# Two of the three modulation parts computed by VectorE from transposed weights, x^T loaded last, experts' biases split on 128 partitions

## The chip, the core and the metric

One core of a Trainium2 chip runs the whole kernel in one launch. The metric is the device time of a launch in microseconds (us). The kernel before takes 1138.96 us (median of 3 runs, 1138.25 to 1139.63).

## The reference

One decoder layer on 256 tokens of width 1024, all in float32. Six vectors of width 1024 (a shift, a scale and a gate for each half of the layer) come from a condition vector `c`; they modulate the inputs of a token mixer and of a mixture of 32 experts, of which each token takes 4.

```
mod = silu(c) @ w_ada + b_ada                    # 1024 -> 6 * 1024
sh_a, sc_a, g_a, sh_f, sc_f, g_f = split(mod, 6)
h   = x * (1 + sc_a) + sh_a
mix = hybrid_mixer(h, w_in, ...)                 # sparse attention and retention, then w_out
x   = layer_norm(ALPHA * x + (1 + g_a) * mix)
h   = x * (1 + sc_f) + sh_f
ff  = moe(h, w_router, w_gate_up, b_gate_up, w_down, b_down)   # top 4 of 32 experts
out = layer_norm(ALPHA * x + (1 + g_f) * ff)
```

## The kernel before

The kernel has a head (modulation, mixer, router) and a body (the 32 experts, whose 12 MB of weights each are streamed from HBM). All large loads are issued by SyncE (SP) in program order as tiles of 128 x 2048 floats, 1 MB each. In the head they go through a ring of 6 buffers (`rtile`, name `w`): a load is issued only when the tile that had the buffer before has been read. In the body 17 buffers (the ring and 11 others, most of which are scratch space of the head) take the experts' tiles in turn. TensorE (PE), VectorE (DVE), ScalarE (ACT) and GpSimd (POOL) each work through a queue of their own in a fixed order, which a scheduler sets at build time from the program order and estimated times; only the end of the kernel and TensorE's part of the router are written out by hand.

**Modulation.** `w_ada` (1024 x 6144) is cut into three parts of 2048 columns and each part into 8 row blocks of 128 (`mod_step(part, k)`). A step loads a 1 MB tile and multiplies it on TensorE with the condition: 4 matmuls of 512 columns into four row groups of one PSUM bank (`pm`). `mod_row` adds the bias, and `mod_cols` transposes the row on TensorE (`pmt`), since the shift and the scale are wanted as one number for each channel, with channels on partitions. Part 0 (shift and scale of the mixer) is needed before anything else: its 8 tiles are loaded first, with x^T behind the sixth. Parts 1 and 2 are spread through the head by `mod_next`, two steps (MODS) ahead of a tile of `w_in`.

**Projections.** x^T (`xT`) is modulated to `h` and split into a rounded part `hh` and a rest `hl` (fp32r). Each tile of `w_in` is split too (`split`): ScalarE makes the rounded part `whi`, VectorE the rest `wlo` (GpSimd for tiles 2, 6 and 10). A projection is three groups of matmuls, `whi` with `hh`, `whi` with `hl`, `wlo` with `hh`, so that its last third waits for `wlo`. There is a small first tile (`w_idx`, 544 columns) and 12 tiles of `w_in`: tile 0 for the index queries, 1 and 2 for the attention queries (`pq`), 3 for keys and values (`pk`), 4 to 7 for the retention queries and keys (`pr`, `rotary`), 8 to 11 for its values and gate (`pv`). Beside them VectorE does the scores (L350), the choice of 64 keys of 256 by eight rounds of MAX and MATCH_REPLACE for each token block (L356, L357), the rotary products (L398 to L401), and the softmax. Then come the output projection (`pz`, 4 tiles of `w_out`), the layer norm and the router (`pg` gathers the tokens for the first experts).

**Biases of the experts.** `bias_rows` loads the biases three times over on 96 partitions and splits them into three bfloat16 parts with one conversion by ScalarE and four instructions by VectorE for each of the two tensors.

Of the kernel before, what the change touches and what calls it, by code (L numbers as in the profile page):

```python
# [23 lines left out]
MODS = 2  # L24
# [4 lines left out]
def layouts(inputs):  # L29
# [20 lines left out]
    head = np.concatenate([ident, cols(g["c"]), cols(g["b_ada"][:2048])], 1)  # L50
# [24 lines left out]
    for c in (2116, 2628):  # L75
# [18 lines left out]
def layer(ctx, tc, t, out):  # L94
# [41 lines left out]
    small(out=dec, in_=t["row"])  # L136
# [5 lines left out]
    ones = sb("ones", 128, 128, pool=keep)  # L142
    G.memset(ones, 1.0)
# [3 lines left out]
    G.memset(epsc, EPS)  # L147

# [6 lines left out]
    b_ada = sb("b_ada", 128, 2, 512)  # L155
    G.memset(b_ada, 0.0)

    def mod_step(part, k, w=None):
        if k == 0:
            mods[part] = ps("s", name="pm")  # L160
        pm = mods[part]
        w = rtile() if w is None else w
        load(out=w, in_=t["w_ada"][0, k * 128:(k + 1) * 128, part * 2048:(part + 1) * 2048])
        for j in range(4):
            mm(pm[32 * j:32 * j + 32], cT[:, k], w[:, j * 512:(j + 1) * 512], k == 0, k == 7)

    def mod_row(part):
        row = sb("modrow", 128, 512, pool=keep)
        if part:
            V.tensor_add(row, mods[part], b_ada[:, part - 1])  # L170
        else:
            V.tensor_copy(row[:, 0:256], mods[part][:, 0:256])
            first["mod"] = A.activation(row[:, 256:512], mods[part][:, 256:512], AF.Copy)
        return row

    def mod_cols(row, lo, n):
        pt = ps("t", (128, 4, 128), name="pmt")
        for b in range(4):
            T.transpose(pt[:, b], row[:, b * 128:(b + 1) * 128], ident)
        return pt.rearrange("p b (j q) -> p j b q", q=32)[:, lo:lo + n, :, 0]  # L180
# [10 lines left out]
    V.tensor_copy(f8, pf[0:8, 0:384])  # L191
# [23 lines left out]
    cst = sb("cst", 128, 1072)  # L215
    below, acausal = cst[:, 0:128], cst[:, 128:256]
    cos, sin = cst[:, 256:512], cst[:, 512:768]
    lnc, w_rt, b_rt = cst[:, 768:784], cst[:, 784:1040].rearrange("p (k e) -> p k e", k=8), cst[0:1, 1040:1072]
    rows_ = sb("rows_", 128, 512, pool=keep)

    xT = spare("xT", 10).rearrange("p (k t) -> p k t", k=8)
    for k in range(8):
        mod_step(0, k, None if k < 6 else spare("w", k - 6))
        if k == 5:
            load(out=xT, in_=t["xT"].rearrange("p (k t) -> p k t", k=8))


    ca = mod_cols(mod_row(0), 0, 4)
    sha, sc1 = sb("sha", 128, 2, 4), sb("sc1", 128, 2, 4)
    bs = b_sa.rearrange("p (j b) -> p j b", b=4)  # L230
    V.scalar_tensor_tensor(sc1, ca[:, 2:4], 1.0, bs[:, 2:4], op0=OP.add, op1=OP.add)
    V.tensor_add(sha, ca[:, 0:2], bs[:, 0:2])
    sc1, sha = [v.rearrange("p a b -> p (a b)") for v in (sc1, sha)]
    hh = spare("hh", 0, F32R).rearrange("p (k t) -> p k t", k=8)
    hl = spare("hl", 1, F32R).rearrange("p (k t) -> p k t", k=8)
    for b in range(8):
        if b % 2 == 0:
            A.activation(hh[:, b], xT[:, b], AF.Identity, bias=sha[:, b:b + 1], scale=sc1[:, b:b + 1])
        else:
            first["h"] = V.tensor_scalar(hh[:, b], xT[:, b], sc1[:, b:b + 1], sha[:, b:b + 1], op0=OP.mult, op1=OP.add)  # L240
    for b in range(0, 8, 2):
        f2 = sb("hfull", 128, 2, 256, bufs=2, tag="zT")
        V.tensor_scalar(f2[:, 0], xT[:, b], sc1[:, b:b + 1], sha[:, b:b + 1], op0=OP.mult, op1=OP.add)
        A.activation(f2[:, 1], xT[:, b + 1], AF.Identity, bias=sha[:, b + 1:b + 2], scale=sc1[:, b + 1:b + 2])
        V.tensor_sub(hl[:, b:b + 2], f2, hh[:, b:b + 2].bitcast(F32))

    queue = [(p, k) for p in (1, 2) for k in range(8)]

    def mod_next(n=1):
        for p, k in queue[:n]:  # L250
            mod_step(p, k)
        del queue[:n]


    nsplit = [0]

    def split(w):
        i = nsplit[0]
        nsplit[0] += 1
        n = w.shape[1]  # L260
        hi = spare("whi", 2 + 2 * (i % 2), F32R)[:, 0:n]
        lo = spare("wlo", 3 + 2 * (i % 2), F32R)[:, 0:n]
        first["split"] = A.activation(hi, w, AF.Copy)  # L263
        (G if i % 4 == 3 and i < 13 else V).tensor_tensor(lo, w, hi.bitcast(F32), op=OP.subtract)  # L264
        return hi, lo
# [41 lines left out]
    w = rtile()[:, 0:544]  # L307
    load(out=w, in_=t["w_idx"])
    with tc.issue_after(first["mod"].ins), tc.issue_after(first["h"].ins):
        w = [d.rearrange("p (k c) -> p k c", k=8) for d in split(w)]  # L310
# [21 lines left out]
    V.tensor_scalar(wi, pw[:, 0:8], 0.0625, None, op0=OP.mult)  # L332
    score = []
# [39 lines left out]
    mod_next()  # L373
# [16 lines left out]
    def rotary(dst):  # L390
        for b2 in range(2):
            mod_next(MODS)
# [587 lines left out]
    for e in range(E - 1):  # L980
# [166 lines left out]
```

## Time and profile before

| | |
|---|---|
| median of 3 runs | 1138.96 us |
| the profiled execution | 1137.54 us, of it 1135.9 us span |
| busy share of the span | PE 92%, PEld 39%, DVE 32%, ACT 16%, POOL 4% |
| mean granted clock of TensorE | 0.981 |
| moved by DMA | 451.99 MB, mean 398 GB/s |
| chain that ended last | DMA 57%, PE 36%, DVE 4%, ACT 1% |

The chain is the profile's walk back from the last instruction, at each step to what released it. Its latest long stretch, from 459 us to 1100 us, is the DMA of the experts' weights; what stands before it is mainly matmuls. A busy TensorE is not TensorE at its peak, since its matmuls are pipelined and their ends modelled; the idle time in front of an instruction and what ended it say more.

### The profile page before, as it was taken

Reading aid. Unit: us, or ns where it says so; the run is one execution under the profiler, and the core shown is the slowest. Engines: PE = TensorE matmul, PEld = TensorE weight load, DVE = VectorE, ACT = ScalarE, POOL = GpSimd, SP = SyncE. Lnnn points to the kernel's source line nnn. Section 1 sums busy time; section 2 is a strip of 40 time slices with the busy share of each in tenths; the row PEclk is TensorE's granted clock in tenths of the full one; section 3 lists DMA queues with packets and bytes.
Section 4 is the critical chain, followed back from the end, with each engine's and each line's share of the span. In section 5 each row is a group of like instructions: output and inputs, shape, how many; then the busy total and the mean of one; then the engine's idle time right before and its main releaser. Section 6 shows DMA issues by size and latency. Waiting matters only on the chain.

```text
span 1135.9 us, 12046 instructions
## 1 busy us (share of the span) xinstructions
PE 1044.3 (92%) x4939; PEld 440.9 (39%) x4939; DVE 360.4 (32%) x661; ACT 177.4 (16%) x292; POOL 49.4 (4%) x38
## 2 busy tenths in 40 slices
PE   7999999999999999999999899989988689999895
PEld 1776676344334333433333233323422233233232
DVE  0676786123122222221322122212221212212125
ACT  1534634101101000100110001000100001100001
POOL 0124110300000000000000000000000000000001
PEclk9899999999899999999999999999999889999998
DMA  9988995999999999999999999999999999999993
GB/s 381 364 320 303 382 385 226 369 421 421 420 422 420 422 420 422 420 422 421 422 421 420 421 421 422 421 422 420 421 421 421 421 419 421 421 421 421 421 416 139
DMA packets 65861, 451.99 MB, mean 398 GB/s; under 512 B 7380, under 2 KB 8573, under 8 KB 11817
## 3 DMA queue, kind: packets, MB, share of 16 engines
q1 hardware_dynamic: 63536, 447.52, 95.6%
q10 hardware_dynamic: 2266, 3.65, 1.0%
q8 instruction: 41, 0.67, 0.2%
q14 instruction: 18, 0.15, 0.0%
HBM read 450.05 MB, written 1.09 MB: 397 GB/s over the span
## 4 chain that ended last, share of the span: by engine, by line
DMA 57%; PE 36%; DVE 4%; ACT 1%; issue 1%; SPq 0%; ACTq 0%; DVEq 0%
DMA w<-in_w_gate_up 37%; DMA w<-in_w_down 19%; PE py L110 7%; PE pgate L110 7%; PE pup L110 6%; PE pm L110 3%; PE pr L110 2%; PE pv L110 2%; PE pz L110 2%; PE pg L110 1%; PE psc L110 1%; PE pb L110 1%; PE pq L110 1%; PE pact L879 1%; DVE wlo L264 1%
## 5 line engine op out<-in xcount | busy, mean ns | idle before, releaser
L110 PE MATMUL pgate<-w,xe 128*64 128x512 f32 x1024 | 341.4, 604 | 24.5 <-DMA w<-in_w_gate_up 24.4
L110 PE MATMUL pup<-w,xe 128*64 128x512 f32 x1024 | 347.4, 594 | 0.0
L110 PE MATMUL py<-w,aT 128*64 128x512 f32 (+1 forms) x1056 | 244.5, 592 | 10.2 <-DMA w<-in_w_down 8.4
L110 PEld LDWEIGHTS pup<-w,xe 128*64 128x64 f32 x1024 | 101.2, 137 | 148.5 <-issue 144.7
L110 PEld LDWEIGHTS pgate<-w,xe 128*64 128x64 f32 x1024 | 90.5, 136 | 173.4 <-issue 92.5
L851 DVE TENSOR_SCALAR sw_g<-pgate 128x512 f32<-128x512 f32 x32 | 22.1, 692 | 396.7 <-PE pgate L110 396.7
L110 PEld LDWEIGHTS py<-w,aT 128*64 128x64 f32 x1056 | 72.0, 137 | 134.3 <-issue 90.4
L897 DVE TENSOR_TENSOR y<-py,gf 64x512 f32<-64x512 f32 x62 | 42.7, 689 | 194.9 <-PE py L110 194.5
L852 ACT ACTIVATE act<-sw_g 128x512 f32<-128x512 f32 x32 | 20.1, 630 | 487.5 <-DVE sw_g L851 487.5
L924 DVE TENSOR_TENSOR acc<-acc,psc 128x512 f32<-128x512 f32 x60 | 38.6, 684 | 23.5 <-PE psc L110 23.5
L1076 POOL TENSOR_TENSOR acc<-acc,ln 128x512 f32<-128x512 f32 (+1 forms) x2 | 2.7, 1342 | 903.5 <-ACT acc L1075 903.5
L803 DVE TENSOR_SCALAR xe<-pg,ha,hb 128x128 f32<-128x128 f32 x64 | 25.7, 409 | 49.6 <-PE pg L110 36.4
L880 ACT ACTIVATE aT<-pact 128x512 f32<-128x512 f32 x32 | 19.1, 597 | 119.9 <-PE pact L879 119.9
L263 ACT ACTIVATE whi<-w 128x2048 fp32r<-128x2048 f32 (+1 forms) x17 | 31.3, 1840 | 34.9 <-DMA w<-lay_w_in 16.3
L804 ACT ACTIVATE xe<-pg,hb,ha 128x128 f32<-128x128 f32 x64 | 28.5, 457 | 47.6 <-DVE xe L803 47.6
L110 PE MATMUL pm<-w,cT 128*32 128x512 f32 x192 | 35.6, 677 | 0.0
L110 PE MATMUL psc<-yh,ohT 128*128 128x512 f32 x60 | 25.4, 464 | 10.9 <-ACT yh L911 7.8
L110 PE MATMUL pg<-oh,nh 128*128 128x256 f32 x128 | 34.8, 306 | 0.5 <-DVE oh L656 0.3
L911 ACT ACTIVATE yh<-y,gs 128x1024 fp32r<-128x1024 f32 x15 | 17.2, 1148 | 107.1 <-DVE y L897 107.1
L110 PEld LDWEIGHTS <-pick 96*64 96x64 bf16 x190 | 15.2, 109 | 47.0 <-issue 44.7
L110 PE MATMUL pg<-oh,nl 128*128 128x256 f32 x128 | 33.4, 293 | 0.0
L264 DVE TENSOR_TENSOR wlo<-w,whi 128x2048 fp32r<-128x2048 f32 (+1 forms) x14 | 30.4, 2172 | 6.4 <-ACT whi L263 6.4
(262 smaller groups left out, 857.1 us busy)
## 6 DMA issues: line engine op xcount, KB each, us to landing
w<-in_w_gate_up SPq DMA_DIRECT2D x256, 1024.0 KB, 19.8
w<-in_w_down SPq DMA_DIRECT2D x124, 1024.0 KB, 19.8
w<-in_w_ada SPq DMA_DIRECT2D x24, 1024.0 KB, 6.9
w<-lay_w_in SPq DMA_DIRECT2D x12, 1024.0 KB, 8.8
w<-lay_w_out SPq DMA_DIRECT2D x4, 1024.0 KB, 11.3
w<-in_w_down SPq DMA_DIRECT2D x7, 512.0 KB, 12.7
xT<-lay_xT SPq DMA_DIRECT2D x1, 1024.0 KB, 14.5
x<-in_x SPq DMA_DIRECT2D x2, 512.0 KB, 10.5
```

The costliest lines, as they stand in the source:

```text
L110: T.matmul(o, l, r, start=start, stop=stop)
L263: first["split"] = A.activation(hi, w, AF.Copy)
L264: (G if i % 4 == 3 and i < 13 else V).tensor_tensor(lo, w, hi.bitcast(F32), op=OP.subtract)
L803: return V.tensor_scalar(xes[h][:, i], src, ha[:, i:i + 1], hb[:, i:i + 1], op0=OP.mult, op1=OP.add)
L804: return A.activation(xes[h][:, i], src, AF.Identity, bias=hb[:, i:i + 1], scale=ha[:, i:i + 1])
L851: V.tensor_scalar(g, pg, 7.0, None, op0=OP.min)
L852: A.activation(s, g, AF.Sigmoid, scale=1.702)
L879: T.transpose(pa[:, 2 * i + j], act[:, 256 * i + j:256 * i + j + 255:2], ident)
L880: A.activation(aT, pa, AF.Copy)
L897: V.tensor_mul(y[o:o + CAP, c], py[64 * c:64 * c + 64], gf[64 * c:64 * c + 64, c * 512:(c + 1) * 512])
L911: A.activation(yh, y, AF.Copy, scale=gs)
L924: V.tensor_add(o, o, p_)
```

## The change

Weights and biases are laid out in another way, and four of the six vectors change engine. `lay_ada_t` holds the columns of the shifts and scales transposed: a tile (128 x 2048) holds 2 x 128 output columns on the partitions with their 1024 weights along the free axis. VectorE multiplies such a row by the condition, which `cB` holds on all partitions, and sums the product in one SCALAR_TENSOR_TENSOR instruction with an accumulator output, two for a tile (`mod_sums`); the sum for each channel lands in a column of `mcol`, so that no transposition is needed. The two gates stay on TensorE (`mod_step`, 8 tiles of `lay_ada_g`, into one `pm`). The tiles of the mixer's shift and scale are loaded first, the last two in halves; `w_idx` is loaded and split ahead of x^T, and x^T in two halves behind all of them. `cB` is made at the start: `c` is loaded as one row, spread to 128 partitions by two matmuls with a row of ones, and passed through Silu by ScalarE. The biases of the experts are split on 128 partitions (5 instructions of VectorE on 768 columns), written to DRAM and read back in the layout of 96 partitions by three loads on ScalarE's queue.

```diff
-    head = np.concatenate([ident, cols(g["c"]), cols(g["b_ada"][:2048])], 1)
+    head = np.concatenate([ident, cols(g["c"]), cols(g["b_ada"][:2048]), cols(g["b_ada"][3072:5120])], 1)
...
+    biases = np.concatenate([gu, dn], 1).reshape(32, 4, 768).transpose(1, 0, 2).reshape(128, 768)
+    wa = np.asarray(inputs["w_ada"])[0]
+    wt = wa.T.reshape(6, 8, 128, 1024)[[0, 1, 3, 4]].reshape(16, 2, 128, 1024).transpose(0, 2, 1, 3)
+    wg = np.concatenate([wa[:, 2048:3072], wa[:, 5120:6144]], 1).reshape(8, 128, 2048)
...
+    crow = scr7[0:1, 2:4].rearrange("p i c -> p (i c)")
+    small(out=crow, in_=t["c"])
...
+    cB = sb("cB", 128, 1024)
+    for j in range(2):
+        pc = ps("s", name="pc")
+        mm(pc, ones[0:1], crow[:, j * 512:(j + 1) * 512])
+        A.activation(cB[:, j * 512:(j + 1) * 512], pc, AF.Silu)
...
+    def mod_tile(i, w=None, pieces=1):
+        w = rtile() if w is None else w
+        n = 2048 // pieces
+        for p in range(pieces):
+            load(out=w[:, p * n:(p + 1) * n], in_=t["ada_t"][i, :, p * n:(p + 1) * n])
+        return w
+
+    def mod_sums(i, w):
+        for b in range(2):
+            wb = w[:, b * 1024:(b + 1) * 1024]
+            V.scalar_tensor_tensor(wb, wb, 1.0, cB, op0=OP.mult, op1=OP.mult,
+                                   accum_out=mcol[:, 2 * i + b:2 * i + b + 1])
...
+    for i in range(8):
+        mod_sums(i, mod_tile(i, None if i < 6 else spare("w", i - 6), 1 if i < 6 else 2))
+        if i == 5:
+            load(out=dec, in_=t["row"])
+        if i == 6:
+            w_first = rtile()[:, 0:544]
+            load(out=w_first, in_=t["w_idx"])
+    for p in range(2):
+        load(out=xT[:, 4 * p:4 * p + 4], in_=t["xT"].rearrange("p (k t) -> p k t", k=8)[:, 4 * p:4 * p + 4])
...
-    ca = mod_cols(mod_row(0), 0, 4)
-    sha, sc1 = sb("sha", 128, 2, 4), sb("sc1", 128, 2, 4)
...
+    w_first = split(w_first)
+    V.tensor_add(sha, mcol[:, 0:8], b_sc[:, 0:8])
+    first["mod"] = V.scalar_tensor_tensor(sc1, mcol[:, 8:16], 1.0, b_sc[:, 8:16], op0=OP.add, op1=OP.add)
...
-    queue = [(p, k) for p in (1, 2) for k in range(8)]
+    queue = list(range(8))
+    queue_t = list(range(8, 16))
...
         for b2 in range(2):
-            mod_next(MODS)
+            mod_next()
+            mod_cols()
             w = w_in("p (k c) -> p k c", k=8)
...
-    b_gu = bias_rows("bias_gu", 4, pool=keep, tag="nn")
-    b_dn = bias_rows("bias_dn", 2, tag="k4a")
+    raw, bpart = btmp[:, 0:768], btmp[:, 768:1920].bitcast(BF16).rearrange("p (o c) -> p o c", o=3)
+    small(out=raw, in_=t["biases"])
+    for o in range(3):
+        V.tensor_copy(bpart[:, o], raw)
+        if o < 2:
+            V.tensor_sub(raw, raw, bpart[:, o])
+    bd = dram.tile([3, 128, 768], BF16, name="bd")
+    small(out=bd.rearrange("o p c -> p o c"), in_=bpart)
+    b_all = sb("b_all", 96, 3072, pool=keep, dt=BF16)
+    for o in range(3):
+        small(out=b_all[32 * o:32 * o + 32].rearrange("r (u c) -> r u c", u=4),
+              in_=bd[o].rearrange("(u r) c -> r u c", u=4))
```

Three places of the engines' queues follow. First VectorE's queue at the first modulation, before: L172 takes the row from PSUM, L231 and L232 form scale and shift from the transposed row, L240 makes the odd blocks of `hh`.

```order
L191 COPY scr_69<-ps_t 8x384
L153 COPY cT<-sg 128x256
L172 COPY modrow<-pm 128x256
L231 SCALAR_TENSOR_TENSOR sc_177<-pmt,head 128x8
L232 TENSOR_TENSOR sha<-pmt,head 128x8
L240 TENSOR_SCALAR hh<-xT,sc_177,sha 128x256 x4
```

The same place of VectorE's queue in the changed kernel; L182 are the sums, L229 is the rest of `w_idx`.

```order
L166 COPY cT<-sg 128x256
L182 SCALAR_TENSOR_TENSOR w,mcol<-w,cB 128x1024 x8
L258 TENSOR_TENSOR sha<-mcol,head 128x8
L182 SCALAR_TENSOR_TENSOR w,mcol<-w,cB 128x1024 x6
L229 TENSOR_TENSOR wlo<-w,whi 128x544
L182 SCALAR_TENSOR_TENSOR w,mcol<-w,cB 128x1024 x2
L259 SCALAR_TENSOR_TENSOR sc_170<-mcol,head 128x8
L266 TENSOR_SCALAR hh<-xT,sc_170,sha 128x256 x4
```

Sixteen sums and the split of `w_idx` now stand in front of `hh`, where one copy and two short instructions stood.

Second, VectorE's queue before, around the rest `wlo` of tile 5 of `w_in` (L264), in the last rounds of the second token block's choice of keys; L398 to L401 are the rotary products of tile 4, of which `pr` is the projection.

```order
L356 MAX best<-score_354 128x8
L357 MATCH_REPLACE score_354<-best,score_354 128x256
L356 MAX best<-score_354 128x8
L357 MATCH_REPLACE score_354<-best,score_354 128x256
L358 TENSOR_SCALAR score_354<-score_354 128x256
L264 TENSOR_TENSOR wlo<-w,whi 128x2048
L398 TENSOR_TENSOR scr_70<-pr,cst 128x512
L400 TENSOR_TENSOR rot<-pr,cst 64x512
L401 TENSOR_TENSOR rot<-pr,cst 64x512
```

The same place in the changed kernel, where L229 is tile 5's `wlo` and L421 to L424 are tile 4's rotary products.

```order
L378 MAX best<-score_345 128x8
L379 MATCH_REPLACE score_345<-best,score_345 128x256
L182 SCALAR_TENSOR_TENSOR w,mcol<-w,cB 128x1024
L378 MAX best<-score_345 128x8
L182 SCALAR_TENSOR_TENSOR w,mcol<-w,cB 128x1024
L379 MATCH_REPLACE score_345<-best,score_345 128x256
L421 TENSOR_TENSOR scr_70<-pr,cst 128x512
L380 TENSOR_SCALAR score_345<-score_345 128x256
L423 TENSOR_TENSOR rot<-pr,cst 64x512
L424 TENSOR_TENSOR rot<-pr,cst 64x512
L229 TENSOR_TENSOR wlo<-w,whi 128x2048
```

Two sums and the rotary products of tile 4 moved ahead of tile 5's `wlo`; two more pairs of sums stand the same way ahead of the `wlo` of tiles 3 and 4.

Third, GpSimd's queue before, from the `wlo` of tile 2 on; L415 adds the bias to the scores for a softmax, L402 ends a rotary product, and the second L264 is the `wlo` of tile 6.

```order
L264 TENSOR_TENSOR wlo<-w,whi 128x2048
L415 TENSOR_TENSOR scr_69<-bias,score_315 128x2x128 x2
L402 TENSOR_TENSOR rot<-rot,scr_70 128x512
L264 TENSOR_TENSOR wlo<-w,whi 128x2048
L402 TENSOR_TENSOR rot<-rot,scr_70 128x512
L415 TENSOR_TENSOR scr_69<-bias,score_315 128x2x128 x2
```

The same place of GpSimd's queue in the changed kernel.

```order
L229 TENSOR_TENSOR wlo<-w,whi 128x2048
L438 TENSOR_TENSOR scr_69<-bias,score_306 128x2x128 x2
L425 TENSOR_TENSOR rot<-rot,scr_70 128x512
L438 TENSOR_TENSOR scr_69<-bias,score_306 128x2x128 x2
L425 TENSOR_TENSOR rot<-rot,scr_70 128x512
L229 TENSOR_TENSOR wlo<-w,whi 128x2048
```

Tile 6's `wlo` went behind the second pair of bias additions and behind the rotary addition of tile 5.

## Rows read from the trace of the kernel before

**Rows 1.** Windows: us, PE, PEld, DVE, ACT, POOL busy (x), PEclk, DMA share, GB/s.
```profile
170.00:180.00 10.00, 10.00 (x60) 8.60 (x59) 7.16 (x19) 3.24 (x5) 0.00 (x0) 1.00 0.19 75
...
192.00:220.00 28.00, 28.00 (x114) 9.71 (x111) 8.17 (x30) 10.60 (x18) 5.04 (x3) 0.94 0.81 323
220.00:1100.00 880.00, 815.91 (x3634) 295.46 (x3630) 211.84 (x353) 88.21 (x151) 4.26 (x2) 0.99 1.01 421
```
**Rows 2.** Waits of SyncE's queue up to 240 us: us in total, times, longest.
```profile
SPq L775 <- PE pup L110: 20.5, 9, 9.8
```
**Rows 3.** Waits of PE, 40 to 191 us: the longest of seven.
```profile
PE pz L110 <- DVE wlo L264: 1.1, 1, 1.1
```
**Rows 4.** Lines of PE by form, 44 to 141 us: xcount, busy us, mean ns, idle.
```profile
L110 PE MATMUL pm<-w,cT 128*32 128x512 f32 x128 | 21.8, 600 | 0.0
```
**Rows 5.** Timeline of PE: start us, us, instruction, xcount.
```profile
79.11 1.12 PE L110 MATMUL pr<-hh,wlo 128*128 128x256 f32 x8
...
89.94 0.64 PE L110 MATMUL pr<-hh,wlo 128*128 128x256 f32 x4
...
98.81 0.39 PE L110 MATMUL pr<-hh,whi 128*128 128x256 f32 x1
...
148.60 0.60 PE L179 MATMUL pmt<-head,modrow 128*128 128x128 f32 x4
...
191.36 1.08 PE L110 MATMUL pgate<-w,xe 128*64 128x512 f32 x4
```
**Rows 6.** Timeline of the start, all engines.
```profile
6.49 0.21 ACT L151 ACTIVATE sg<-head 128x8 f32<-128x8 f32 x1 [2.90 <-DMA head<-lay_head]
...
16.50 2.07 PE L110 MATMUL ps_t<-scr,ones 1*128 1x512 f32 x2
...
18.60 0.60 ACT L214 ACTIVATE scr<-ps_t 128x512 f32<-128x512 f32 x1 [3.47 <-PE ps_t L110]
...
30.07 1.39 DVE L240 TENSOR_SCALAR hh<-xT,sc,sha 128x256 fp32r<-128x256 f32 x4
```
**Rows 7.** Timeline of DVE: instructions with two SBUF inputs, one with the accumulator.
```profile
182.65 1.27 DVE L653 SCALAR_TENSOR_TENSOR nl<-acc,lsd,nh 128x1024 fp32r<-128x1024 f32 x1
183.83 0.20 DVE L627 BATCH_NORM_AGGREGATE lmv<-lst 128x2 f32<-128x12 f32 x1
...
195.30 0.19 DVE L714 SCALAR_TENSOR_TENSOR gate<-gate,msk 128x32 f32<-128x32 f32 x1 [2.07 <-ACT gate L713]
195.41 0.08 DVE L714 DVE_READ_ACCUMULATOR gate<-gate,msk 128x1 f32 x1
...
196.48 0.22 DVE L723 SCALAR_TENSOR_TENSOR late<-rk,gate 128x64 f32<-128x64 f32 x1
```
**Rows 8.** Timeline of DVE: tile 5's rest, and the next wait for PE.
```profile
73.14 2.28 DVE L264 TENSOR_TENSOR wlo<-w,whi 128x2048 fp32r<-128x2048 f32 x1
...
83.22 0.69 DVE L398 TENSOR_TENSOR scr<-pr,cst 128x512 f32<-128x512 f32 x1 [5.77 <-PE pr L110]
```
**Rows 9.** Lines of DVE by form, 28 to 191 us: the score products.
```profile
L350 DVE SCALAR_TENSOR_TENSOR score<-scr,wi,score 128x128 f32<-128x128 f32 x4 | 5.6, 1388 | 0.1
...
L350 DVE SCALAR_TENSOR_TENSOR score<-scr,wi,score 128x256 f32<-128x256 f32 x4 | 1.9, 467 | 0.0
```
**Rows 10.** Timeline of POOL.
```profile
48.89 4.64 POOL L264 TENSOR_TENSOR wlo<-w,whi 128x2048 fp32r<-128x2048 f32 x1 [6.06 <-ACT whi L263]
...
86.23 1.27 POOL L402 TENSOR_TENSOR rot<-rot,scr 128x512 f32<-128x512 f32 x1
```
**Rows 11.** Windows round two short waits of PE, columns as in Rows 1.
```profile
182.00:184.00 2.00, 1.10 (x9) 0.90 (x9) 1.97 (x5) 0.60 (x1) 0.00 (x0) 1.00 1.05 442
...
186.00:188.00 2.00, 2.00 (x12) 2.00 (x11) 1.55 (x3) 0.30 (x1) 0.00 (x0) 0.50 1.04 438
```
**Rows 12.** The page's DMA issues: xcount, KB each, us to landing.
```profile
raw_bias_gu<-lay_bias_gu ACTq DMA_DIRECT2D x1, 768.0 KB, 7.9
```

More of the change, by code (lines that the diff above doesn't have):

```diff
@@ L135, in layer @@
     dec = scr9[0:1]
-    small(out=dec, in_=t["row"])
+    ones = sb("ones", 128, 128, pool=keep)
+    G.memset(ones, 1.0)
+    cB = sb("cB", 128, 1024)
[3 more added lines that the diff above has]
+        A.activation(cB[:, j * 512:(j + 1) * 512], pc, AF.Silu)
     ident_r = sb("ident_r", 128, 128, pool=keep, dt=F32R)
@@ L154, in layer, with mod_step @@
     mods, first = {}, {}
-    b_ada = sb("b_ada", 128, 2, 512)
+    b_ada = sb("b_ada", 128, 512)
     G.memset(b_ada, 0.0)
-    def mod_step(part, k, w=None):
+    mcol = sb("mcol", 128, 32)
+    def mod_tile(i, w=None, pieces=1):
[9 more added lines that the diff above has]
+                                   accum_out=mcol[:, 2 * i + b:2 * i + b + 1])
+    def mod_step(k):
         if k == 0:
[L160 to L163, printed above, removed]
+            mods["g"] = ps("s", name="pm")
+        w = rtile()
+        load(out=w, in_=t["ada_g"][k])
         for j in range(4):
[L165 to L180, printed above, removed]
+            mm(mods["g"][32 * j:32 * j + 32], cT[:, k], w[:, j * 512:(j + 1) * 512], k == 0, k == 7)
     def bcast_row(dst, row, j, add):
@@ L214, in layer @@
     A.activation(retg, pb, AF.Copy)
[L215 to L225, printed above, removed]
-    ca = mod_cols(mod_row(0), 0, 4)
-    sha, sc1 = sb("sha", 128, 2, 4), sb("sc1", 128, 2, 4)
[L230 to L233, printed above, removed]
+    w_first = split(w_first)
+    sha, sc1 = sb("sha", 128, 8), sb("sc1", 128, 8)
+    V.tensor_add(sha, mcol[:, 0:8], b_sc[:, 0:8])
+    first["mod"] = V.scalar_tensor_tensor(sc1, mcol[:, 8:16], 1.0, b_sc[:, 8:16], op0=OP.add, op1=OP.add)
     hh = spare("hh", 0, F32R).rearrange("p (k t) -> p k t", k=8)
@@ L237, in layer, with mod_cols @@
         if b % 2 == 0:
-            A.activation(hh[:, b], xT[:, b], AF.Identity, bias=sha[:, b:b + 1], scale=sc1[:, b:b + 1])
+            first["hA"] = A.activation(hh[:, b], xT[:, b], AF.Identity, bias=sha[:, b:b + 1], scale=sc1[:, b:b + 1])
         else:
[L240 to L245, printed above, removed]
-    queue = [(p, k) for p in (1, 2) for k in range(8)]
+            first["hV"] = V.tensor_scalar(hh[:, b], xT[:, b], sc1[:, b:b + 1], sha[:, b:b + 1],
+                                          op0=OP.mult, op1=OP.add)
+    with tc.issue_after(first["hA"].ins), tc.issue_after(first["hV"].ins):
+        for b in range(0, 8, 2):
+            f2 = sb("hfull", 128, 2, 256, bufs=2, tag="zT")
+            V.tensor_scalar(f2[:, 0], xT[:, b], sc1[:, b:b + 1], sha[:, b:b + 1], op0=OP.mult, op1=OP.add)
+            A.activation(f2[:, 1], xT[:, b + 1], AF.Identity, bias=sha[:, b + 1:b + 2], scale=sc1[:, b + 1:b + 2])
+            V.tensor_sub(hl[:, b:b + 2], f2, hh[:, b:b + 2].bitcast(F32))
+    queue = list(range(8))
+    queue_t = list(range(8, 16))
     def mod_next(n=1):
-        for p, k in queue[:n]:
-            mod_step(p, k)
+        for k in queue[:n]:
+            mod_step(k)
         del queue[:n]
[L255 to L265, printed above, removed]
+    def mod_cols(n=1):
+        for i in queue_t[:n]:
+            mod_sums(i, mod_tile(i))
+        del queue_t[:n]
     ntile = [0]
@@ L304, in back @@
         return blocks(a)[:, :, ::-1]
[L307 to L310, printed above, removed]
+    w = [d.rearrange("p (k c) -> p k c", k=8) for d in w_first]
     pk = ps("g")
```

71 lines of the change are left out of this document (40 added, 31 removed).

## The prediction

> **What bounds the kernel now.** I read the windows first, then the waits of SyncE's queue, then the timelines of TensorE (PE), VectorE (DVE) and GpSimd (POOL) in the head. The windows show two regimes. From 220 to 1100 us the DMA is full at 421 GB/s; before that it is not: 0.19 busy from 170 to 180 us and 0.81 from 192 to 220 us [rows 1]. In these holes SyncE waits for buffers that TensorE's first experts still hold [rows 2]. So the end is the moment at which the stream of experts runs freely plus a fixed amount of data, and what the head gains or loses until the first expert matmul at 191.36 us [rows 5] goes to the end one to one. The bytes stay: the same 24 MB of `w_ada`, and 0.4 MB more on the way of the biases, which fall in a stretch where the DMA has holes.
>
> In the head TensorE sets the pace. From 40 to 191 us its longest wait is 1.1 us [rows 3], and its modulation steps cost 21.8 us for 128 instructions, 8 to a step, so 16 steps of 1.36 us [rows 4]. VectorE is close behind: its queue has its first long wait for TensorE, 5.77 us, only after the `wlo` of tile 5 of `w_in` [rows 8]. The change takes work from the first and gives it to the second, so the sum has to follow VectorE's queue.
>
> **The first modulation.** Before, `hh` starts at 30.07 us [rows 6]. Now 16 sums stand in front of it. The trace has no sum of this width with an accumulator; it has the same instruction on 1024 columns with two SBUF inputs, 1.18 us from its start to the next start, and the reading of an accumulator, 0.08 us [rows 7]: 1.26 us a sum, 20.2 us in all. To it come the rest of `w_idx` (a quarter of the columns of the 2.28 us in [rows 8], 0.6 us) and two tiny instructions, 0.3 us. The sums begin when `cB` is there. `c` is the first transfer on ScalarE's queue, as `head` was, which landed at 6.49 us; each spreading matmul costs the 2.07 us of the pair in [rows 6], the second Silu 0.60 us. With a landing of the 4 KB at 5.3 us the sums begin at 5.3 + 4.1 + 0.6 = 10.0 us. Ends: 11.2 us if it lands as late as `head`; 7.2 us if it lands so early that the copy of `cT` behind `head` decides. `hh` starts at 10.0 + 21.1 = 31.1 us, 1.0 us later than before (from 1.8 us earlier to 2.2 us later). The 9.9 MB up to the end of x^T take 23.5 us at the rate of [rows 1] and are there before the sums are done, so x^T's place behind the weights costs nothing; its early place before bought nothing either.
>
> [...]
>
> **VectorE from there to tile 5.** Before, the `wlo` of tile 5 ends at 73.14 + 2.28 = 75.4 us [rows 8] and TensorE takes it up at 79.11 us [rows 5]: it had 3.7 us to spare. Now the queue starts 1.0 us later, and ahead of this instruction stand three pairs of sums (6 x 1.26 = 7.6 us) and the three rotary products of tile 4 (3 x 0.69 = 2.1 us). No idle time lies in that stretch to take them, so the `wlo` ends at 75.4 + 1.0 + 7.6 + 2.1 = 86.1 us and TensorE takes it up at 86.2 us, 7.1 us late. The three modulation steps that TensorE no longer has there buy nothing: their 4.1 us and the 7.1 us are what it waits for the `wlo` of tiles 3, 4 and 5, some 3.7 us each. One thing is not in the sum: a sum and an addition of GpSimd may block each other, as the products of [rows 9] show, where the narrow ones took 1388 ns in the mean and the wide ones 467 ns, while GpSimd's 4.64 us split ran [rows 10]. For the scores this is so in both kernels; for the sums I take 0, with 4.6 us as the upper end.
>
> **GpSimd and tile 6.** TensorE needs 83.22 - 79.11 = 4.1 us to end tile 5 [rows 5, 8]: 90.3 us. The three products take 2.1 us, 92.4 us. GpSimd's queue now has tile 5's rotary addition (1.27 us) in front of tile 6's `wlo` (4.64 us) [rows 10]: 98.3 us. TensorE takes it up at 98.4 us in place of 89.94 us, 8.5 us late. From there to tile 7 it took 8.9 us (98.81 us [rows 5]), with two modulation steps; now there is one, and tile 7 starts at 105.9 us, 7.1 us late.
>
> **From tile 7 to the first expert.** Seven modulation steps stood here, four are left: -3 x 1.36 = -4.1 us. The two groups of transposes `pmt` go, 0.6 us each with overlap [rows 5], so -1.0 us. Tile 7's `wlo` comes 2.1 + 2.28 = 4.4 us after tile 6's end, and TensorE has 3.4 us of work before it needs it (a modulation step of 1.36 us and two groups of 8 matmuls, 1.0 us each by [rows 5]): +1.0 us. From here VectorE has air: the biases cost it 5 instructions on 768 columns in place of 8 on 1024 or 2048, beside matmuls in both kernels, and the router's weights (w_ha, w_hb) are made earlier. That leaves 7.1 - 4.1 - 1.0 + 1.0 = +3.0 us.
>
> **The clock.** [...] I take 1.5 us, between 0 and 4 us.
>
> **The biases' detour** through DRAM stands on ScalarE's queue: three loads wait for a write, and ScalarE's next split with them. A load of similar size took 7.9 us [rows 12]. The matmuls of the last `pv` tile and of the retention behind it cover it as far as they reach; I take 0, with half of the 7.9 us, 4 us, as the upper end.
>
> **The sum.** +3.0 + 1.5 = +4.5 us: the first expert matmul at about 195.9 us, the profiled execution at 1137.54 + 4.5 = 1142.0 us. The median of the runs stands 1.4 us above that execution, so 1143.4 us.
>
> **The rivals.**
>
> *TensorE stays the bound.* If the sums find room in VectorE's waits, TensorE keeps what it saves: 8 x 1.36 = 10.9 us and the 1.0 us of transposes, less 1.0 us at the start, 1138.96 - 10.9 = 1128.1 us; if waits eat half of it, 1133.5 us. For it speaks that TensorE hardly waits [rows 3] and that VectorE has a hole of 5.77 us [rows 8]; against it, that the hole lies behind the instruction that is late, in a queue that keeps its order. Chance 0.2.
>
> *It comes out even.* `c` lands early (-2.8 us) and the clock holds (-1.5 us): 4.5 - 4.3 = +0.2 us, 1139.2 us. Chance 0.2.
>
> *ScalarE stands in the detour* (+4 us): 1147.4 us. For it speaks that the write waits for a subtraction with two SBUF inputs beside GpSimd's split of tile 10. Chance 0.13.
>
> [...] Chance 0.07.
>
> **How the numbers follow.** The forecast, slower by 4.5 us with VectorE's queue as the cause, has 0.40; its own range is 1140 to 1148 us. About 0.2% (2.3 us) is what a measurement of this kernel tells from no change. Slower: 0.40 + 0.13 + 0.07 = 0.60. Same: 0.20. Faster: 0.20. The range of 8 in 10 goes from 1132 us, within the first rival, to 1151 us, beyond the detour; it leaves out the half rate (0.07), the better half of the first rival (0.1) and the tails.
>
> **What would show it.** Right: `hh` at about 31 us; TensorE waiting 3 to 4 us each in front of the last third of tiles 3, 4 and 5 with VectorE's `wlo` as the releaser, and of tile 6 with GpSimd's; sums of 1.2 to 1.3 us; a granted clock of 0.5 after such waits; the first expert matmul near 196 us, and nothing new after 220 us. Wrong: TensorE without waits and a first expert before 189 us (the first rival); sums over 2 us; `hh` before 29 us; or a stream of experts that ends later or earlier than its start moved.

## The result, and the profile after

The changed kernel takes 1159.55 us in the median of 4 runs (1156.48 to 1160.15), beside 1138.61 us for the kernel before: a ratio of 1.0177, 95% interval 1.0158 to 1.0197. Forecast were 1143.4 us. The sign was right and the size was not: +20.9 us where +4.5 were worked out, outside the range of 1132 to 1151. The profiled execution took 1156.48 us with a span of 1154.9 us; it is the shortest of the four, 3.1 us under their median, and has the highest mean granted clock (0.982; the others 0.977 and 0.978).

The windows of the changed kernel, in the columns of [rows 1]:

```profile
90.00:100.00 10.00, 3.87 (x22) 3.35 (x19) 8.68 (x12) 1.86 (x8) 8.21 (x4) 0.66 0.73 265
...
120.00:130.00 10.00, 5.19 (x21) 4.09 (x20) 4.04 (x10) 4.47 (x10) 1.89 (x1) 0.86 0.59 240
...
192.00:220.00 28.00, 25.43 (x150) 15.27 (x150) 15.15 (x52) 12.09 (x19) 0.00 (x0) 1.00 0.71 279
220.00:1100.00 880.00, 812.83 (x3621) 294.34 (x3617) 212.69 (x360) 91.29 (x157) 9.30 (x4) 0.99 1.01 419
```

TensorE, which hardly paused before, stands still for about half of two stretches of 10 us; its mean granted clock in them is 0.66 and 0.86. The last row is the surprise behind 220 us: the DMA is as full as in [rows 1], but moves 419 GB/s and not 421.

TensorE's waits from 40 to 210 us (engine, tile, line, waited for: us in total, times, longest), where [rows 3] had 1.1 us at most:

```profile
PE pp L456 <- DVE scr L452: 10.9, 4, 4.8
PE pr L115 <- DVE wlo L229: 6.1, 3, 2.5
PE pk L115 <- DVE wlo L229: 2.5, 1, 2.5
PE pa L115 <- ACT scr L476: 1.9, 1, 1.9
```

The second and third were forecast. The first, the largest, is the softmax: `pp` are the transposes of the probabilities, which wait for VectorE's product with the reciprocal sum (L452). The prediction did not name it.

TensorE's timeline at the places of [rows 5], and the two waits of over 4 us:

```profile
84.39 1.22 PE L115 MATMUL pr<-hh,wlo 128*128 128x256 f32 x8 [2.53 <-DVE wlo L229]
...
97.05 0.47 PE L456 MATMUL pp<-head,scr 128*128 128x128 f32 x1 [4.00 <-DVE scr L452]
...
100.33 0.76 PE L115 MATMUL pr<-hh,wlo 128*128 128x256 f32 x5
...
105.68 1.22 PE L115 MATMUL pr<-hh,whi 128*128 128x256 f32 x8
...
127.64 1.12 PE L456 MATMUL pp<-head,scr 128*128 128x128 f32 x4 [4.81 <-DVE scr L452]
...
207.15 1.08 PE L115 MATMUL pgate<-w,xe 128*64 128x512 f32 x4
```

Tile 5's last third comes 5.3 us late, tile 7 6.9 us late, and then, instead of winning back the 4.1 us that were worked out, the first expert matmul is 15.8 us late (207.15 against 191.36). The span grew by 19.0 us; the other 3.2 us are lost behind the first expert.

Where the 4.00 us come from, on GpSimd and VectorE:

```profile
92.42 4.49 POOL L229 TENSOR_TENSOR wlo<-w,whi 128x2048 fp32r<-128x2048 f32 x1
...
92.64 4.54 DVE L452 TENSOR_SCALAR scr<-scr,sm 128x128 f32<-128x128 f32 x2
```

Two small products, 0.48 us a pair where nothing disturbs them, last as long as GpSimd's split of tile 6 beside them. Late as VectorE is, they now meet this split.

Where the 4.81 us and the 1.9 us come from, on ScalarE, VectorE and GpSimd:

```profile
117.30 4.59 POOL L438 TENSOR_TENSOR scr<-bias,score 128x512 f32<-128x512 f32 x2
...
121.92 0.36 ACTq L534 DMA_DIRECT2D btmp<-lay_biases  x1
...
123.51 0.17 DVE L450 RECIPROCAL sm<-sm 128x2 f32<-128x2 f32 x1 [2.77 <-ACT scr L448]
...
126.76 0.56 DVE L536 CAST btmp<-btmp 128x768 bf16<-128x768 f32 x1 [3.09 <-DMA btmp<-lay_biases]
127.24 0.61 DVE L452 TENSOR_SCALAR scr<-scr,sm 128x256 f32<-128x256 f32 x2
...
136.37 5.72 POOL L229 TENSOR_TENSOR wlo<-w,whi 128x2048 fp32r<-128x2048 f32 x1 [14.48 <-ACT whi L228]
...
137.66 4.86 DVE L536 CAST btmp<-btmp 128x768 bf16<-128x768 f32 x1
...
142.54 0.38 ACTq L540 DMA_DIRECT2D bd<-btmp  x1
143.03 1.92 ACT L228 ACTIVATE whi<-w 128x2048 fp32r<-128x2048 f32 x1 [3.34 <-DVE btmp L536]
...
151.47 1.36 ACTq L543 DMA_DIRECT2D b_all<-bd  x3
...
152.95 1.91 ACT L228 ACTIVATE whi<-w 128x2048 fp32r<-128x2048 f32 x1 [8.01 <-PE pv L115]
```

Read them as a chain. The biases' load can only start when `bias`, whose buffer it takes over, has been read for the last time, by GpSimd's additions L438 (121.9 us). VectorE's first cast of the biases stands in its queue ahead of the softmax products and waits for that load; the products, whose inputs are ready at 123.7 us, come at 127.24 us. TensorE had waited since 122.8 us, so some 1.2 of the 4.81 us are not the cast's. The third cast meets GpSimd's split of tile 10 and lasts 4.86 us instead of 0.56 us, so the write to DRAM leaves at 142.54 us. ScalarE's queue then stands at the three loads that wait for this write until 151.47 us; its next split begins at 152.95 us. The row names `pv` as the releaser, but `whi`'s last reader was done at 150.3 us: it was the queue.

### The profile page after: what moved, and what is told of

The parts are those of the page before. It is cut to its first block, busy times and chain, and to the rows that moved or that the text cites. A ratio compares the mean times of both kernels' runs of the same rounds, so it can differ in the third digit from the quotient of the medians.

```text
span 1154.9 us, 11840 instructions
## 1 busy us (share of the span) xinstructions
PE 1024.5 (89%) x4803; PEld 437.4 (38%) x4803; DVE 398.4 (34%) x718; ACT 175.3 (15%) x292; POOL 56.2 (5%) x38
## 5 line engine op out<-in xcount | busy, mean ns | idle before, releaser
L115 PE MATMUL pgate<-w,xe 128*64 128x512 f32 x1024 | 338.0, 606 | 29.5 <-DMA w<-in_w_gate_up 29.5
L922 DVE TENSOR_TENSOR y<-py,gf 64x512 f32<-64x512 f32 x62 | 42.7, 689 | 193.7 <-PE py L115 193.3
L182 DVE SCALAR_TENSOR_TENSOR w<-w,cB 128x1024 f32<-128x1024 f32 x32 | 40.7, 1314 | 0.5 <-ACT cB L150 0.5
L229 DVE TENSOR_TENSOR wlo<-w,whi 128x2048 fp32r<-128x2048 f32 (+1 forms) x14 | 30.5, 2177 | 12.0 <-ACT whi L228 11.9
L115 PE MATMUL psc<-yh,ohT 128*128 128x512 f32 x60 | 25.0, 457 | 10.6 <-ACT yh L936 7.3
L228 ACT ACTIVATE whi<-w 128x2048 fp32r<-128x2048 f32 (+1 forms) x17 | 31.1, 1838 | 20.1 <-PE pv L115 8.0
```

Source lines behind the costliest of these rows:

```text
L115: T.matmul(o, l, r, start=start, stop=stop)
L182: V.scalar_tensor_tensor(wb, wb, 1.0, cB, op0=OP.mult, op1=OP.mult, accum_out=mcol[:, 2 * i + b:2 * i + b + 1])
L922: V.tensor_mul(y[o:o + CAP, c], py[64 * c:64 * c + 64], gf[64 * c:64 * c + 64, c * 512:(c + 1) * 512])
```

## The experiments

All were timed beside the kernel before on the same chip, in four sittings, in which it took 1137.87, 1137.44, 1137.90 and 1136.31 us (1138.61 beside the changed kernel). So runs of different sittings are compared by their distance to the kernel before beside them; the changed kernel's is +20.9 us, and the intervals of the ratios are some 2 us to either side. Theory A: the price is where the biases' chain stands in the queues of VectorE and ScalarE, on top of the sums. Rival B: the sums are all of it, and another wait would take the chain's place.

**Old biases in the changed kernel.** `bias_rows` of before in place of L532 to L546.

```diff
-    btmp = sb("btmp", 128, 2048, pool=keep, tag="nn")
...
+    b_gu = bias_rows("bias_gu", 4, pool=keep, tag="nn")
+    b_dn = bias_rows("bias_dn", 2, tag="k4a")
```

> The changed kernel with the experts' biases loaded and parted as before (three copies on 96 partitions, no detour through DRAM). Theory A, the bias chain stands in the queues of VectorE and ScalarE and costs about 9 of the 21 us: TensorE's wait of 4.8 us at 122.8 and the 1.9 us before pa go, first expert matmul near 198 instead of 207.2, time 1147 to 1153. Rival B, the 16 sums behind the first tiles cost it all and another wait takes the place of the bias chain's: 1156 to 1161.

Measured: 1153.14 us, +15.3 us, ratio 1.0131 (1.0102 to 1.0160). The wait of 4.8 us is gone, and 5.7 us with it, less than theory A's 9. The first expert matmul came at 203.9 us, not 198: the old biases are more work on VectorE (174.1 us busy up to 220 us, 164.2 in the changed kernel), and TensorE now waits 1.4 us for the decay product and 1.1 us for the modulation's row behind them.

**The parted biases alone**, in the kernel before: the same edit the other way round.

> The kernel before with the parting of the biases on 128 partitions and the detour through DRAM as the only edit. Theory A: the cast waits for its load at the head of VectorE's queue, and ScalarE's queue for the write; 4 to 9 us more, 1143 to 1148. Rival B: the chain is hidden, 1138 to 1140.

Measured: 1155.20 us, ratio 1.0153 (1.0124 to 1.0182). More than either theory allowed: alone this part costs 17 us, nearly as much as the whole change. VectorE's timeline:

```profile
118.20 0.56 DVE L513 CAST btmp<-btmp 128x768 bf16<-128x768 f32 x1 [4.99 <-DMA btmp<-lay_biases]
...
119.67 0.61 DVE L430 TENSOR_SCALAR scr<-scr,sm 128x256 f32<-128x256 f32 x2
...
125.50 5.44 DVE L430 TENSOR_SCALAR scr<-scr,sm 128x256 f32<-128x256 f32 x4
```

The same cast waits 4.99 us ahead of the same products. The next products, late by it, meet GpSimd's split of tile 10 (126.24 to 130.78 us) and last 5.44 us. In the profiled execution (1148.77 us, the shortest of six) TensorE waits 7.4 us for softmax products, 4.8 of them at the first place and 2.2 at the second, and the first expert matmul is 10.6 us late. What the longer runs lose beyond that, no trace shows.

**Only the first modulation by VectorE.** The second one's shift and scale by TensorE in eight more steps, old biases.

```diff
-    queue = list(range(8))
-    queue_t = list(range(8, 16))
+    queue = [(p, k) for p in "cg" for k in range(8)]
```

> Only the first modulation by VectorE with x^T last; shift and scale of the second by TensorE in 16 steps with the gates, biases as before. Theory A (the sums cost only where VectorE is full, from 56 to 113 us): hh 0.6 us late and the rest as before, 1138 to 1142. Rival B (sums cost by their number, 16 of 32 stay): 1144 to 1150.

Measured: 1143.38 us, ratio 1.0053 (1.0036 to 1.0071): between the two. The head is as theory A has it (first expert matmul at 192.3 us, 0.9 us late), yet the time is 5.5 us longer: the rest is lost behind it, at 419 to 420 GB/s.

**Late sums.** Old biases, and the sums of tiles 10 to 15 behind the splits of the `pv` tiles.

```diff
-            mod_cols()
             w = w_in("p (k c) -> p k c", k=8)
...
             hi, lo = w_in("p (k c) -> p k c", k=4)
+            mod_cols(2 - half)
```

> As the changed kernel with the old biases, but the sums of tiles 10 to 15 taken from the stretch of the rotary tiles to that of the four pv tiles, behind the splits. Theory A: tile 5 and the softmax after it go as before, the loss there of some 5 us goes, 1142 to 1148. Rival B (sums cost the same wherever they stand): as with the old biases alone, 1147 to 1153.

Measured: 1145.69 us, ratio 1.0056 (1.0035 to 1.0077), 7.5 us less than with the old biases alone. The place of the sums counts, and not their number alone: without them the rotary tiles end early, and the first `pv` tile starts at 107.8 us (before 110.8, changed kernel 118.2).

**The ring's place.** In all four kernels with the changed kernel's head tile the expert stage ran at 419 to 420 GB/s; in both others at 421. That tile is 64 bytes wider, and the ring, which lies behind it, moves with it. The bytes given here are the places in the built programs; no trace shows them. So the kernel before got an unused tile ahead of the ring, of 64, 96 and 32 bytes.

```diff
     slots = sb("slots", 128, CAP, pool=keep)
+    pad = sb("pad", 128, 16, pool=keep)   # 24 in the second, 8 in the third
+    G.memset(pad, 0.0)
```

> The kernel before with an unused tile of 64 bytes per partition ahead of the ring, so that the ring's 17 buffers begin at byte 46560 of a partition, as in the changed kernel, and not at 46496 (the changed kernel's head tile is 64 bytes wider). Every kernel with the ring at 46560 moved 419 to 420 GB/s from 300 to 1000 us, both with it at 46496 moved 421. Theory R, the place of the ring sets the rate: 419 to 420 GB/s, 1141 to 1142 us. Rival: the rate goes with other inputs in DRAM or the order of loads; 421 GB/s, 1137 to 1139 us.

> The same with 96 bytes, so that the ring begins at byte 46592, a multiple of 512. Theory R: a rate of its own, at least 421 GB/s if whole multiples of 512 are good, 1134 to 1138 us; or 419 if any place after 46496 is worse, 1141. Rival: 421 GB/s, 1137 to 1139 us.

> The kernel before with 32 unused bytes ahead of the ring, whose buffers then begin at byte 46528: a multiple of 64, not of 512 (46496, 46560 and 46592 gave 421, 419 to 420 and 427 GB/s). If a multiple of 64 is enough: 427 GB/s and 1125 to 1129 us. If it takes more than that, 421 GB/s or less, 1136 to 1141.

Windows from 300 to 1000 us, one fence a kernel: before, changed, and 64, 96 and 32 bytes:

```profile
300.00:1000.00 700.00, 645.95 (x2883) 231.62 (x2881) 168.93 (x284) 72.73 (x125) 0.00 (x0) 0.99 1.01 421
```
```profile
300.00:1000.00 700.00, 639.33 (x2844) 228.81 (x2843) 168.47 (x284) 70.17 (x122) 0.00 (x0) 0.99 1.01 420
```
```profile
300.00:1000.00 700.00, 643.92 (x2869) 230.64 (x2867) 169.21 (x285) 72.74 (x125) 0.00 (x0) 0.99 1.01 419
```
```profile
300.00:1000.00 700.00, 650.12 (x2911) 234.64 (x2909) 170.63 (x287) 72.73 (x125) 0.00 (x0) 0.99 1.01 427
```
```profile
300.00:1000.00 700.00, 644.35 (x2874) 230.75 (x2872) 170.24 (x286) 72.20 (x124) 0.00 (x0) 0.99 1.01 421
```

Everything behind the unused tile moves with it, but what these loads fill are the ring's buffers. Times: 64 bytes 1139.70 us, ratio 1.0026 (1.0010 to 1.0042); 96 bytes 1126.63 us, ratio 0.9904 (0.9887 to 0.9921); 32 bytes 1135.68 us, ratio 1.0001 (0.9985 to 1.0017). Theory R holds for the rate: the DMA is busy all the time in each (1.01), and what it moves, 419 to 427 GB/s, depends on where the buffers begin. The times were missed, by 1.3 us with 64 bytes, by 7 us with 96 and by 0.3 us with 32, all to the short side. At 46528, a multiple of 64, the rate is still 421 GB/s; at 46592, a multiple of 512, it is 427, 1.4% more. With 64 and 96 bytes the first expert matmul is also 2.3 to 2.4 us later, mostly by a wait for the decay product (1.9 and 1.4 us). The kernel with 32 bytes, the same but for the size of the unused tile, has no such wait. With 64 and 96 bytes ScalarE had waited 3.2 and 3.8 us for a tile of `w_in`, with 32 bytes 1.9; why the tile came later is not shown. So 2 us in the head of a single execution say little. The kernel before with 96 unused bytes is the fastest measured here, 10.8 us under the kernel before.

**The changed kernel with its ring at a multiple of 512** (32 unused bytes).

> The changed kernel with 32 unused bytes ahead of the ring, whose buffers then begin at byte 46592 of a partition, a multiple of 512, as in the run that made the kernel before 11 us faster. Theory R: 427 GB/s instead of 419 to 420 from 300 us on, that is 1.7% of some 880 us, 12 to 15 us less: 1144 to 1148. Rival (TensorE's lateness bounds it, the rate is not used): 1152 to 1160.

Measured: 1143.24 us, +5.3 us, ratio 1.0048 (1.0030 to 1.0066), at 427 GB/s. It gains 15.6 us where 12 to 15 were worked out, and its time is 0.8 us below the expected 1144 to 1148; the rival falls.

**Early biases**, parted by ScalarE and GpSimd in the head, the detour on GpSimd's queue.

```diff
+    G.dma_start(out=raw, in_=t["biases"])
+    for o in range(3):
+        A.activation(bpart[:, o], raw, AF.Copy)
+        if o < 2:
+            G.tensor_sub(raw, raw, bpart[:, o])
```

> The changed kernel with the biases loaded at the start, parted by ScalarE and GpSimd before 30 us and sent through DRAM on GpSimd's queue, so that neither the work nor the waits stand in VectorE's or ScalarE's queues after 100 us. Theory A: the waits of 4.8 us at 122.8 and of 1.9 us before pa go with their low clock, the 7 us up to the first pv tile stay: first expert matmul 196 to 200 (207.2 before the edit), 1146 to 1152. Rival B (another wait takes their place): 1156 to 1161.

Measured: 1153.32 us, ratio 1.0145 (1.0126 to 1.0165). Both waits are gone, but the expected time was missed by 1 us and the first expert matmul (204.9 us) by 5, since `hh` came 4 us late. The sums began 1.05 us later (11.15 us), and the rows show where another 2.9 went:

```profile
14.19 1.97 POOL L210 TENSOR_TENSOR btmp<-btmp 128x768 f32<-128x768 f32 x1 [11.40 <-ACT btmp L208]
...
17.12 1.63 POOL L210 TENSOR_TENSOR btmp<-btmp 128x768 f32<-128x768 f32 x1 [0.96 <-ACT btmp L208]
```
```profile
14.59 2.65 DVE L182 SCALAR_TENSOR_TENSOR w<-w,cB 128x1024 f32<-128x1024 f32 x1
...
17.17 2.66 DVE L182 SCALAR_TENSOR_TENSOR w<-w,cB 128x1024 f32<-128x1024 f32 x1
...
19.76 1.21 DVE L182 SCALAR_TENSOR_TENSOR w<-w,cB 128x1024 f32<-128x1024 f32 x1
```

Beside each of GpSimd's two subtractions one sum lasts 2.65 us instead of 1.2. So this run takes one cost away and adds another, and does not decide between theory A and rival B.

**Late biases.** The same parted biases, with the casts behind the product with the decay and the detour on GpSimd's queue.

```diff
-    for o in range(3):
+    with tc.issue_after(first["pa"].ins):   # V.tensor_mul(at[:, :, 256:384], pa, ...)
...
-    small(out=bd.rearrange("o p c -> p o c"), in_=bpart)
+    G.dma_start(out=bd.rearrange("o p c -> p o c"), in_=bpart)
```

> The changed kernel with the same parted biases, but the casts placed on VectorE behind the product with the decay (L498) and the detour through DRAM on GpSimd's queue; the load stays where it is. Theory A (the price is the place of the chain in the in-order queues, not its work): no wait of 4.8 us at 122.8, none before pa, hh at 30 as in the changed kernel; first expert matmul 195 to 200 instead of 207.2, 1147 to 1152. Rival B: 1156 to 1161.

Measured: 1150.95 us, +13.1 us, ratio 1.0112 (1.0094 to 1.0131), 7.9 us less with the same instructions. VectorE's casts in it:

```profile
L584 DVE CAST btmp<-btmp x3: 527/551/561, 161.8 to 168.5; 128x768 bf16<-128x768 f32 x3
```

They come 35 us later, and no wait of TensorE is put down to them. Theory A stands: the place cost, not the work. Since this edit moves the casts and the detour together, it does not part what each cost. The first expert matmul, 201.3 us, is 1.3 us later than expected, as the first `pv` tile started at 120.6 us in this execution (118.2 in the changed kernel's).

**Tile 6's lower part by VectorE** in the changed kernel.

```diff
-        (G if i % 4 == 3 and i < 13 else V).tensor_tensor(lo, w, hi.bitcast(F32), op=OP.subtract)
+        (G if i in (3, 11) else V).tensor_tensor(lo, w, hi.bitcast(F32), op=OP.subtract)
```

> The changed kernel with the lower part of w_in tile 6 by VectorE instead of GpSimd. Theory L: the 4.0 us that TensorE waits at 97 for the softmax products, which last 4.54 us for two beside GpSimd's 4.49, go; tile 7 starts 2 to 4 us earlier; 1155 to 1158. Rival: the 2.3 us more on VectorE eat it, 1158 to 1161.

Measured: 1153.04 us, +15.1 us, ratio 1.0138 (1.0117 to 1.0158), 5.8 us less and more than theory L said. On VectorE:

```profile
92.60 0.48 DVE L452 TENSOR_SCALAR scr<-scr,sm 128x128 f32<-128x128 f32 x2
...
93.33 2.28 DVE L229 TENSOR_TENSOR wlo<-w,whi 128x2048 fp32r<-128x2048 f32 x1
```

The products take 0.48 us where they took 4.54, and the split costs VectorE half of what it cost GpSimd. Between the two profiled executions the difference is smaller, 3.5 us of span: tile 7 starts at 103.00 us instead of 105.68. But the changed kernel's execution was a short one. In the traces of three other runs that leave this part as it is (old biases, late biases, ring at a multiple of 512) tile 7 starts at 107.69, 108.02 and 106.57 us.

**Three edits together:** late biases, late sums, ring at a multiple of 512.

> Three edits together: the late biases, the sums of tiles 10 to 15 in the stretch of the pv tiles instead of the rotary tiles, and the ring at a multiple of 512. If theory A, the place of the sums and the rate hold and add: first expert matmul 188 to 194, 427 GB/s, 1119 to 1127, no slower than the kernel before with the ring alone moved (1126.6). If the costs only change places: first expert 196 or later, 1129 to 1136.

Measured: 1130.98 us, ratio 0.9937 (0.9919 to 0.9955): faster than the kernel before, but not than that kernel with 96 unused bytes, and within the second expectation. The first expert matmul stood at 195.6 us: in the `pv` stretch TensorE again waits for VectorE (2.2 us for a softmax product, 1.6 us for the decay product). The gain of the rotary stretch was given back there.

**The three costs undone together:** late biases, tile 6 by VectorE, ring at a multiple of 512.

> The changed kernel with three of the edits that each gained alone: biases late (-8.6 us), tile 6's lower part by VectorE (-6.5), ring at a multiple of 512 (-16.3). If the three costs are separate terms they add: 1126 to 1131, first expert matmul 196 to 200. If the first two are one wait seen twice: 1133 to 1137, first expert matmul 201 or later.

Measured: 1132.90 us, ratio 0.9966 (0.9954 to 0.9977), first expert matmul at 197.4 us. Beside the kernel before it is -3.4 us, 24.4 us less than the changed kernel; the three gains alone add up to 29.3 us (7.9, 5.8 and 15.6). So they are mostly separate; the 4.9 us that are missing are about the noise of such a sum. The time lies between the two expectations, the first expert matmul within the first.

**One table for all.** The span of each profiled execution, less the start of its first expert matmul:

| ring begins at | GB/s | kernels: first expert matmul, rest of the span |
|---|---|---|
| 46496, 46528 | 421 | before 191.4, 944.5; parted biases alone 202.0, 945.2; 32 bytes 190.3, 943.4 |
| 46560 | 419 to 420 | changed 207.2, 947.7; old biases 203.9, 948.3; first modulation only 192.3, 948.5; late sums 195.8, 948.8; 64 bytes 193.8, 946.5; early biases 204.9, 948.7; late biases 201.3, 949.3; tile 6 204.3, 947.1 |
| 46592 | 426 to 427 | 96 bytes 193.7, 933.7; changed 206.9, 933.4; both late 195.6, 934.7; three undone 197.4, 934.1 |

The rest is the same within 3 us in a row of the table, whatever the head does, and the head of the changed kernel is the same at either rate (207.2 and 206.9). These are the two numbers that make the time. (The rest of the kernel with 64 bytes is 2.0 us above the kernel before's, the changed kernel's 3.2.)

## Why the prediction was right or wrong

**The frame: right, and it lacked a term.** The end does move one to one with the first expert matmul, for each rate by itself (the rest of the span is the same within 3 us). The prediction took the rate as given ("nothing new after 220 us") and so missed the ring's 2 to 3 us.

**The first modulation: right number, by luck at its start.** The sums start at 10.10 us (forecast 10.0), and not for the reason given:

```profile
2.44 3.75 PE L115 MATMUL pc<-scr,ones 1*128 1x512 f32 x4 [2.44 <-DMA scr<-lay_c]
...
8.88 0.21 ACT L164 ACTIVATE sg<-head 128x8 f32<-128x8 f32 x1 [5.27 <-DMA head<-lay_head]
...
9.00 1.06 ACT L150 ACTIVATE cB<-pc 128x512 f32<-128x512 f32 x2
...
10.10 1.22 DVE L182 SCALAR_TENSOR_TENSOR w<-w,cB 128x1024 f32<-128x1024 f32 x1 [0.47 <-ACT cB L150]
...
11.25 1.22 DVE L182 SCALAR_TENSOR_TENSOR w<-w,cB 128x1024 f32<-128x1024 f32 x1
...
30.01 1.38 DVE L266 TENSOR_SCALAR hh<-xT,sc,sha 128x256 fp32r<-128x256 f32 x4
```

`c` had landed by 2.4 us, not at 5.3, and the spreading matmuls were done at 6.2 us. But ScalarE's queue has the Silu of `head` in front, and `head` landed at 8.9 us, 2.4 us later than in [rows 6]. Two errors cancel. The sums take 1.15 us each from start to start (forecast 1.26), and `hh` starts at 30.01 us, as before [rows 6] (forecast 31.1). No run shows sums at half rate, to which the prediction gave 0.07: in the median of all 32 a sum lasts 1.22 us.

**VectorE up to tile 5: right in kind, too large.** TensorE waits 2.5, 2.4 and 2.5 us in front of the last thirds of tiles 3, 4 and 5 (forecast 3.7 each), and takes up tile 5's at 84.39 us (forecast 86.2). The collision of sums with GpSimd's additions, taken as 0, was there: five sums beside GpSimd's additions lasted 1.34 to 2.31 us, 2.6 us more in all than at 1.22 us.

**Tile 6 and 7: right number, wrong reason.** Tile 7 starts at 105.68 us (forecast 105.9; 106.6 to 108.0 in the three other traces named above). But TensorE did not wait for GpSimd's `wlo` of tile 6: it waited for the softmax products that this very split held up. The prediction had looked for such a collision only with the sums and taken 0 for it, with 4.6 us as the upper end; the 4.54 us fell on another instruction. Giving the split to VectorE gained 5.8 us.

**From tile 7 to the first expert: here the forecast failed.** Worked out were -4.1 us, or -2.6 with the clock's 1.5; this stretch became 8.9 us longer (101.5 us, before 92.6). The work on TensorE did shrink: its modulation steps took

```profile
L115 PE MATMUL pm<-w,cT 128*32 128x512 f32 x64 | 10.6, 605 | 0.0
```

where [rows 4] had 21.8 us. But "the biases cost it 5 instructions on 768 columns in place of 8 on 1024 or 2048, beside matmuls in both kernels" counted work, and what cost was a wait: the cast waits for a load that could not start before 121.9 us, and the softmax stood behind it. Before, the first reader of the biases was ScalarE's copy (old L512), behind which no softmax product waited. How much it was shows in the same stretch, from tile 7 to the first expert matmul, of the runs with the chain out of the way, late biases and three costs undone:

```profile
108.02 1.22 PE L115 MATMUL pr<-hh,whi 128*128 128x256 f32 x8
...
201.30 1.08 PE L115 MATMUL pgate<-w,xe 128*64 128x512 f32 x4
```
```profile
104.69 1.19 PE L115 MATMUL pr<-hh,whi 128*128 128x256 f32 x8
...
197.36 1.08 PE L115 MATMUL pgate<-w,xe 128*64 128x512 f32 x4
```

It lasts 93.3 and 92.7 us; with the chain in place 101.5, 100.3 (ring at a multiple of 512) and 101.4 us (tile 6 by VectorE). So the chain is worth 7 to 9 us there. Without it the stretch is as long as before, and not 4.1 us shorter: the saving on TensorE did not show. In the trace with three costs undone, TensorE's waits for other engines in this stretch are 5.9 us against 3.1 in the kernel before; what took the rest is open.

**The biases' detour: taken as 0, it was not.** The step asked what covers ScalarE's wait for DRAM, and the `pv` matmuls do cover most of the 8.9 us from the write to the loads: 1.9 us of TensorE's waits are left. It did not ask what stands at the other end of the chain, on VectorE. Both ends together are worth 7.9 us here, twice the upper end of 4 us; no run parts them.

**The clock: right in kind.** The granted clock is 0.66 in the window of the 4.0 us wait and 0.86 in that of the 4.8 us; before, it was 0.50 in the window from 186 us [rows 11]. It also differs between executions: after the wait for tile 5's `wlo`, the run with old biases shows 0.69 from 85 to 90 us, and the eight matmuls behind it take 2.08 us; in the changed kernel's trace it is 1.00, and they take 1.22 us. No run parts what the clock cost, and none shows the 1.5 us that stand for it in the sum.

**The account.** With the three costs undone, and the ring at the same place as in the fastest kernel, the change is 7.4 us slower (-3.4 and -10.8 us beside the kernel before). In its trace tile 7 is 5.9 us late and the first expert matmul 6.0 us. I put this down to the sums in VectorE's queue, for which the forecast was 4.5; that is argued, since no run leaves out the sums alone. Among the runs with old biases, the one without the second modulation's sums is at +5.5 us and the one with them at +15.3, tile 6's collision included. The ring is worth 2 to 3 us. What is left of the 20.9 us, some 11 us, is the biases' chain and tile 6's split, which alone are worth 7.9 and 5.8.

Open is why the parted biases cost 17 us in the kernel before and half of it in the changed one. One part is in the traces: there the softmax products meet GpSimd's split of tile 10, 2.2 us for TensorE, and in the changed kernel a cast does. That the changed kernel's other waits cover a part is an argument, not shown.

## What to carry to other kernels

Price a new instruction by what it waits for and by who stands behind it in its engine's queue, at every end of its chain, before counting its work. An instruction that comes later meets other neighbours: after moving VectorE's queue, look again at what GpSimd runs beside it (here two products of 0.48 us took 4.54 us beside a split). And when any tile changes its size, look where the large DMA buffers behind it begin (here the rate went from 419 to 427 GB/s with their place).

## What was not expected of the hardware

The rate of a full DMA went with the byte of a partition at which the ring's buffers begin: 421 GB/s at 46496 and 46528, 419 to 420 at 46560, 426 to 427 at 46592. So 427 GB/s is 1.4% above the first two and 1.7 to 1.9% above the third. Only one of the four places gave the higher rate, and no run tells what about it counts.

Beside a GpSimd instruction with two SBUF inputs a VectorE instruction with a single wide one took longer as well: two products of 0.48 us lasted 4.54 us beside a split of 4.49 us, and a cast of 0.56 us lasted 4.86 us beside a split of 5.72 us. The products end 0.27 us behind the split, the cast 0.43 us. No run shows why.
